# Joint softmax statistics in block 1's attention and two-pass state updates in the gated linear attention of a two-block model

## Chip, cores and metric

One core of one Trainium2 chip. The metric is the device time of one execution in microseconds (us), the median of three runs. TensorE (PE) multiplies, VectorE (DVE), ScalarE (ACT) and GpSimd (POOL) work on tiles of 128 partitions, and SyncE (SP) issues the DMAs.

## The reference, cut to what matters

The whole model is a first block (FFN, a mixer of sliding-window attention beside a state-space model, FFN) and a second one (multi-head latent attention, conv-FFN, gated linear attention or GLA, conv-FFN) on 512 tokens of width 1024. The change touches two places. In block 1's attention each query block of 128 tokens sees 16 meta keys and a band of 256 keys, with one sink score per head in the softmax:

```python
q = (q * (HEAD_DIM ** -0.5)).reshape(b, l, N_KV_HEADS, Q_PER_KV, HEAD_DIM)
sc = jnp.einsum('bqkgd,bskd->bkgqs', qn, keys).astype(jnp.float32)
p = sink_softmax(sc, mask, sink)          # softmax over the scores and one sink per head
```

In GLA (4 heads, key width 128, value width 256, 8 chunks of 64 tokens) each chunk updates a state and is read with it:

```python
upd = jnp.einsum('bnchk,bnchv->nbhkv', k_dec, v).astype(jnp.float32)
state = state * g[..., None] + u
return state, jnp.einsum('bchk,bhkv->bchv', qc, state)
```

## The kernel before

Activations lie transposed, features on partitions and tokens along the row. Every large product is made in three matmuls of a type that PE takes in one pass (fp32r): operands are split into a high half, rounded to that type, and a low half, the rest. `fetch` loads a weight tile `raw` on SP's queue, makes `whi` on ACT (L86) and `wlo` on DVE (L66); `wload` hands the next one out, out of rings of five. `proj` (L182) multiplies 512 or 2 x 264 tokens, and `nat` (L198) makes 128 tokens x 256 features: 24 matmuls of 256 columns, which this text calls a chunk of projection. Small products (scores, transposes, states) take plain fp32 operands.

The instructions of each engine are put in order by a scheduler when the program is built; PE, ACT, DVE, POOL and SP then run their own lists in order.

Block 1's attention (from L700): `query` evacuates a projection and scales it by 1/8 and by the token's norm factor `Rr`. A unit is two key heads (`pp`) with four query heads each and one block of 128 queries, eight units in all. `scores1` makes eight score matmuls (L727), evacuates each with a reduction that adds the mask and takes the row maximum (L730), and then, head by head, the maximum with the sink, its negative, the sink's exponential, four exponentials, the sum, its reciprocal and the scaling. `turn1` transposes (L759, L769), `values1` multiplies with the values (L781, L785). The quarters of the state-space model (`ssm_quarter`, L569 to L592) are woven in.

GLA (from L1286): `keys` makes `ek` in place, decayed keys of 128 tokens (two chunks of 64) x 512; `values` evacuates each 128 x 256 piece into `gv` with one copy. `recur` walks a head's four blocks `b`: two state updates (L1370), one for each chunk `c`, with 64 rows of `ek` against 64 rows of `gv`, into two PSUM banks; then the states `S` on DVE (L83) and the reading of each with the queries `gq` (L1381), which here is called the S matmul. The generators in `fill` make the next head's projections between the steps.

Of the kernel before, what the change touches and what calls it, by code (L numbers as in the profile page):

```python
# [53 lines left out]
def body(nc, tc, A, out, es):  # L54
# [10 lines left out]
    def tt(o, a, b, op, e=None):  # L65
        return (e or V).tensor_tensor(o, a, b, op=op)  # L66
# [581 lines left out]
    with tc.tile_pool(name="m1", bufs=1) as mp:  # L648
        att = mp.tile([P, 8, S], F32, name="att")
        with tc.tile_pool(name="m2", bufs=1) as ap_:  # L650
# [65 lines left out]
            def scores1(u):  # L716
# [6 lines left out]
                st = [[sm.tile([P, 4], F32, name=f"at{j}{s_}", bufs=2) for j in range(3)] for s_ in range(2)]  # L723
                for i in range(4):
                    pq = [pss("q"), pss("q")]
                    for s_ in range(2):
                        last["sc"] = PE.matmul(pq[s_][:, :W], qf[pp * 4 + i][:, n * P:(n + 1) * P],  # L727
                                               kw[pp][s_][:, max(n - 1, 0), :W])
                    for s_ in range(2):
                        V.tensor_tensor_reduce(sc[s_][:, i, :W], pq[s_][:, :W], mk, 1.0, -3.0e38,  # L730
                                               ALU.add, ALU.max, st[s_][0][:, i:i + 1])
                for s_ in range(2):
                    mx, dn, nb = st[s_]
                    t = sc[s_]
                    kv = 2 * pp + s_
                    sk = sink[:, kv * 4:kv * 4 + 4]
                    tt(mx, mx, sk, ALU.max)
                    ts(nb, mx, -1.0)
                    sub(mx, sk, mx)
                    act(mx, mx, AF.Exp)  # L740
                    for i in range(4):
                        act(t[:, i, :W], t[:, i, :W], AF.Exp, bias=nb[:, i:i + 1], accum_out=dn[:, i:i + 1])
                    add(dn, dn, mx)
                    V.reciprocal(dn, dn)
                    mul(mt[:, :, 32 * s_:32 * s_ + NM], t[:, :, :NM], dn.unsqueeze(2).to_broadcast([P, 4, NM]))
                    if s_:
                        for i in range(4):
                            act(t[:, i, NM:W], t[:, i, NM:W], AF.Copy, scale=dn[:, i:i + 1])
                    else:
                        mul(t[:, :, NM:W], t[:, :, NM:W], dn.unsqueeze(2).to_broadcast([P, 4, W - NM]))  # L750
                live[u] = sc, mt

            def turn1(u):
# [532 lines left out]
    with tc.tile_pool(name="g1", bufs=2) as mp:  # L1286
# [22 lines left out]
        for t, m in zip(L, lm):  # L1309
            act(t, t, AF.Ln, bias=1.0)  # L1310
            sub(t, m, t)
        ek = []
        for b in range(4):
            p = pss("s")
            PE.matmul(p, gc[:, 0:P], half(L, b))
            t = mp.tile([P, S], F32, name=f"ek{b}", bufs=1)
            act(t, p, AF.Exp)
            ek.append(t)
        pd = pss("s")
        for b in range(4):  # L1320
            for hh in range(4):
# [12 lines left out]

        def queries(i):

            t = qt[i] = mp.tile([P, 4, 2, P], F32, name=f"gq{i}", bufs=1)
# [4 lines left out]
            yield  # L1342

        def values(i):
            t = vt[i] = mp.tile([P, 4, 256], F32, name=f"gv{i}", bufs=1)
            return token("gla_v", lambda b, p: act(t[:, b], p, AF.Copy))

        def keys(c):
            return token("gla_k", lambda b, p: mul(ek[b][:, c * 256:(c + 1) * 256], ek[b][:, c * 256:(c + 1) * 256], p))

        def gates(hh):
            g = rg[hh] = mp.tile([P, 4, 256], F32, name="rg", tag="rg", bufs=4)
# [9 lines left out]
        def recur(hh):  # L1362
# [3 lines left out]
            for b in range(4):  # L1366
                pu = [pss("u"), pss("u")]
                for c in range(2):
                    rows = slice(64 * c, 64 * c + 64)
# [15 lines left out]
        def normalise(hh):  # L1385
            st4 = mp.tile([P, 4, 6], F32, name="st4")
            mv = mp.tile([P, 4, 2], F32, name="mv")
            nm = mp.tile([P, 4], F32, name="nm")
            o = ob[hh] = mp.tile([P, 4, 256], F32, name="ob", bufs=4)
# [188 lines left out]
```

## Time and profile before

| | |
|---|---|
| median of three runs | 2582.53 us (2582.31 to 2583.71) |
| the profiled execution | 2580.72 us, of which its span is 2578.9 us |
| PE busy | 2558.5 us, 99% of the span |
| DVE busy | 1577.0 us, 61% |
| ACT busy | 993.6 us, 39% |
| granted TensorE clock, mean | 0.999 |

Busy time of PE is made of matmul records whose ends are modelled and which overlap: a 256-column matmul's record lasts 0.28 us, while the next one starts 0.12 us later. What one matmul costs is read from the distance between starts.

### The profile page before, as it was taken

The numbers are of one execution on the slowest core, as the hardware profiler recorded it, in microseconds if no ns is written. First come the engines' busy times: TensorE is split into PE (matmuls) and PEld (weight loads), VectorE is DVE, ScalarE is ACT, GpSimd is POOL, SyncE is SP. The second block draws the span as 40 slices with busy tenths as digits, with TensorE's granted clock in tenths as the row PEclk, the third lists the DMA queues.
The fourth block names the chain that finished last, engine by engine and source line by source line (L and its number), as shares of the span: only waits on it lengthen the run. The fifth ranks groups of instructions, "written<-read, shape, count | busy, mean of one in ns | idle before, by whom it ended". The sixth has DMA issues, their size and how long they took to land.

```text
span 2578.9 us, 34903 instructions
## 1 busy us (share of the span) xinstructions
PE 2558.5 (99%) x13914; PEld 2181.4 (85%) x13914; DVE 1577.0 (61%) x2866; ACT 993.6 (39%) x1560; POOL 84.8 (3%) x98
## 2 busy tenths in 40 slices
PE   9999999999999999999999999999999999999999
PEld 9999999766888888888888888888878888888887
DVE  7985445685457544468665775555763457655566
ACT  5222223445333222236554454333353234433333
POOL 0000001000000000000000001000000010100000
PEclk9999999999999999999999999999999999999999
DMA  5443324332333333332112223333232222333332
GB/s 183 132 135 110 97 91 135 105 97 63 105 98 96 97 98 98 98 94 70 54 58 62 75 81 108 97 98 98 82 101 66 74 60 83 120 98 98 98 92 73
DMA packets 80774, 243.64 MB, mean 94 GB/s; under 512 B 10418, under 2 KB 20530, under 8 KB 80483
## 3 DMA queue, kind: packets, MB, share of 16 engines
q1 hardware_dynamic: 80610, 241.40, 30.8%
q8 instruction: 110, 1.80, 0.3%
q14 instruction: 54, 0.43, 0.1%
HBM read 229.44 MB, written 11.93 MB: 94 GB/s over the span
## 4 chain that ended last, share of the span: by engine, by line
PE 97%; DVE 2%; ACT 0%; issue 0%; DMA 0%; SPq 0%; DVEq 0%; ACTq 0%
PE ps_b L182 27%; PE ps_q L182 19%; PE ps_t L182 18%; PE mm L182 16%; PE ps_b L198 5%; PE ps_o L1240 1%; PE ps_q L1212 1%; PE ps_q L727 1%; PE ps_o L785 1%; PE ps_t L1228 1%; PE ps_q L1370 1%; DVE sq L66 1%; DVE h L66 0%; PE ps_t L769 0%; PE ps_b L1443 0%; PE ps_q L198 0%
## 5 line engine op out<-in xcount | busy, mean ns | idle before, releaser
L86 ACT ACTIVATE whi<-raw 128x1024 fp32r<-128x1024 f32 (+2 forms) x418 | 432.6, 1038 | 980.9 <-PE ps_b L182 276.3
L66 DVE TENSOR_TENSOR wlo<-raw,whi 128x1024 fp32r<-128x1024 f32 (+2 forms) x418 | 502.4, 1204 | 328.8 <-ACT whi L86 326.6
L182 PE MATMUL ps_b<-zh,whi 128*128 128x512 f32 (+1 forms) x692 | 272.9, 394 | 2.3 <-ACT att L86 0.7
L182 PE MATMUL ps_b<-zl,whi 128*128 128x512 f32 (+1 forms) x692 | 269.7, 390 | 0.0
L182 PE MATMUL ps_b<-zh,wlo 128*128 128x512 f32 (+1 forms) x692 | 269.1, 389 | 0.0
L182 PE MATMUL ps_q<-zh,whi 128*128 128x512 f32 (+1 forms) x488 | 189.3, 388 | 1.2 <-ACT zh L86 1.2
L182 PE MATMUL ps_q<-zl,whi 128*128 128x512 f32 (+1 forms) x488 | 189.4, 388 | 0.0
L182 PE MATMUL ps_q<-zh,wlo 128*128 128x512 f32 (+1 forms) x488 | 189.2, 388 | 0.0
L182 PE MATMUL ps_t<-zh,whi 128*128 128x512 f32 x476 | 185.6, 390 | 0.6 <-ACT zh L86 0.6
L182 PE MATMUL ps_t<-zl,whi 128*128 128x512 f32 x476 | 185.5, 390 | 0.0
L182 PE MATMUL ps_t<-zh,wlo 128*128 128x512 f32 x476 | 185.2, 389 | 0.0
L182 PE MATMUL mm<-zh,whi 128*128 128x264 f32 x800 | 162.5, 284 | 5.7 <-ACT whi L86 5.7
L182 PE MATMUL mm<-zl,whi 128*128 128x264 f32 x800 | 161.8, 284 | 0.0
L182 PE MATMUL mm<-zh,wlo 128*128 128x264 f32 x800 | 161.2, 283 | 0.0
L182 PEld LDWEIGHTS ps_b<-zh,whi 128*128 128x128 f32 (+1 forms) x692 | 129.2, 187 | 33.8 <-issue 2.5
L182 PEld LDWEIGHTS ps_b<-zh,wlo 128*128 128x128 f32 (+1 forms) x692 | 129.2, 187 | 28.6 <-issue 1.1
L182 PEld LDWEIGHTS ps_b<-zl,whi 128*128 128x128 f32 (+1 forms) x692 | 129.3, 187 | 27.2 <-issue 0.7
L182 PEld LDWEIGHTS mm<-zh,whi 128*128 128x128 f32 x800 | 124.3, 189 | 5.8 <-ACT whi L86 5.7
L182 PEld LDWEIGHTS mm<-zl,whi 128*128 128x128 f32 x800 | 124.1, 189 | 0.3 <-DVE zl L83 0.3
L182 PEld LDWEIGHTS mm<-zh,wlo 128*128 128x128 f32 x800 | 124.0, 189 | 0.0
L182 PEld LDWEIGHTS ps_q<-zh,whi 128*128 128x128 f32 x488 | 91.6, 188 | 20.8 <-ACT zh L86 2.0
L182 PEld LDWEIGHTS ps_q<-zl,whi 128*128 128x128 f32 x488 | 91.6, 188 | 20.4 <-DVE zl L66 1.3
(581 smaller groups left out, 5322.2 us busy)
## 6 DMA issues: line engine op xcount, KB each, us to landing
raw<-in_ffn_w_dram SPq DMA_DIRECT2D x130, 512.0 KB, 3.5
raw<-in_w_up_dram SPq DMA_DIRECT2D x88, 512.0 KB, 3.6
raw<-in_w_down_dram SPq DMA_DIRECT2D x44, 512.0 KB, 3.6
raw<-in_w_in_dram SPq DMA_DIRECT2D x32, 512.0 KB, 3.5
raw<-in_mla_o_dram SPq DMA_DIRECT2D x16, 512.0 KB, 3.6
raw<-in_ple_g_dram SPq DMA_DIRECT2D x16, 512.0 KB, 3.7
raw<-in_glu_dram SPq DMA_DIRECT2D x8, 512.0 KB, 3.5
raw<-in_w_out_dram SPq DMA_DIRECT2D x8, 512.0 KB, 3.5
```

Of the source, the lines that this page charges most:

```text
L66: return (e or V).tensor_tensor(o, a, b, op=op)
L86: return SC.activation(o, a, f, **kw)
L182: last["pe"] = PE.matmul(o[:, i, :c1 - c0], lhs, x[k][r][:, c0:c1], start=(k == 0 and j == 0), stop=(k == kt - 1 and j == 2))
L198: PE.matmul(o[:m, :n], x[k][a][:, t0:t0 + m], w[b][:, kk_ * c + m0:kk_ * c + m0 + n], start=(k == 0 and i == 0), stop=(k == kt - 1 and i = ...
L727: last["sc"] = PE.matmul(pq[s_][:, :W], qf[pp * 4 + i][:, n * P:(n + 1) * P], kw[pp][s_][:, max(n - 1, 0), :W])
L785: PE.matmul(po[64 * s_:64 * s_ + 64], vb[n - 1 + j][:, kv * 64:kv * 64 + 64], pT[s_][:, j], start=False, stop=(j == 1))
L1212: PE.matmul(p[:, :N], d["q"][e][:, bs], d["k"][e][:, :N], start=False, stop=True)
L1228: PE.transpose(pt[:, kt * P:(kt + 1) * P], sc[:, kt * P:(kt + 1) * P], ident)
L1240: PE.matmul(po[:, b * P:(b + 1) * P], vt[:, kt, e * P:(e + 1) * P], pT[:, kt * P:(kt + 1) * P], start=(kt == 0), stop=(kt == b))
L1370: PE.matmul(pu[c][:, :256], ek[b][rows, hc], vt[hh][rows, b])
```

## The change

Block 1. Four weight tiles (keys and values) are fetched ahead of the two key projections. A query is evacuated by an ACT copy with the factor 1/8; the token's norm factor moves into the reduction of the scores, as its factor `r`, and the sink moves in as the reduction's start value. The statistics of both heads of a unit lie in tiles of eight columns, and what follows (negative, exponential of the sink, sum, reciprocal) is done once for both; the maximum with the sink falls away.

GLA. The decayed keys are split: `kd[b][c]` holds, on the 64 partitions of chunk `c`, the high half, and on the other 64 the low half of the same keys. `gvh` holds the values' high half of chunk `c` on all 128 partitions (twice), and the low-half tile `gvl` (a ring of six that is zeroed once) has the low half on 64 partitions and zeros on the other 64. A state update is now two fp32r matmuls over 128 rows (L1399 of the changed program): `kd` against `gvh`, then against `gvl`. The queries' tiles `gq` become a ring of two, `ob` too.

```diff
+            for _ in range(4):
+                fetch("w_in", 1024)
             kw = []
...
-                stt(t, p[:, 0, :], 0.125, Rr, ALU.mult, ALU.mult)
+                act(t, p[:, 0], AF.Copy, scale=0.125)
...
-                        V.tensor_tensor_reduce(sc[s_][:, i, :W], pq[s_][:, :W], mk, 1.0, -3.0e38,
-                                               ALU.add, ALU.max, st[s_][0][:, i:i + 1])
+                        V.tensor_tensor_reduce(sc[s_][:, i, :W], pq[s_][:, :W], mk, r[:, n:n + 1], sk[:, c:c + 1],
+                                               ALU.add, ALU.max, mx[:, c:c + 1])
+                ts(nb, mx, -1.0)
+                sub(mx, sk, mx)
+                act(mx, mx, AF.Exp)
                 for s_ in range(2):
-                    mx, dn, nb = st[s_]
...
-                    tt(mx, mx, sk, ALU.max)
-                    ts(nb, mx, -1.0)
-                    sub(mx, sk, mx)
-                    act(mx, mx, AF.Exp)
                     for i in range(4):
...
-                    add(dn, dn, mx)
-                    V.reciprocal(dn, dn)
...
+                add(dn, dn, mx)
+                V.reciprocal(dn, dn)
...
+        kd = [[mp.tile([P, S], F32R, name=f"kd{b}{c}", bufs=1) for c in range(2)] for b in range(4)]
+        ch = lambda c: slice(64 * c, 64 * c + 64)
+        vl = [mp.tile([P, 2, 256], F32R, name=f"gvl{i}", bufs=1) for i in range(6)]
+        for t in vl:
+            for c in range(2):
+                ts(t[ch(1 - c), c], mask[ch(1 - c), :256], 0.0)
...
-            return token("gla_v", lambda b, p: act(t[:, b], p, AF.Copy))
...
+                for c in range(2):
+                    act(h_[ch(c), c], p[ch(c)], AF.Copy)
+                    act(h_[ch(1 - c), c], p[ch(c)], AF.Copy)
+                    sub(l[ch(c), c], p[ch(c)], h_[ch(c), c].bitcast(F32))
...
+                mul(t, t, p)
+                for c in range(2):
+                    k = kd[b][c][:, cols]
+                    act(k[ch(c)], t[ch(c)], AF.Copy)
+                    sub(k[ch(1 - c)], t[ch(c)], k[ch(c)].bitcast(F32))
...
-                    PE.matmul(pu[c][:, :256], ek[b][rows, hc], vt[hh][rows, b])
+                    for i, t in enumerate(vt[hh][b]):
+                        PE.matmul(pu[c][:, :256], kd[b][c][:, hc], t[:, c], start=(i == 0), stop=(i == 1))
```

Where the rows stand in the lists of the engines. On PE, in head 0's second block, the two updates and an S matmul before:

```order
L198 MATMUL ps_b<-whi,zl_16697 128x256
L198 MATMUL ps_b<-wlo,zh_16696 128x256
L1370 MATMUL ps_q<-gv_16801,ek_16772 128x256
L1381 MATMUL ps_o<-S,gq_16802 128x256
L1370 MATMUL ps_q<-gv_16801,ek_16772 128x256
L198 MATMUL ps_b<-whi,zh_16668 128x256
```

and in the third block now (L1410 is the S matmul):

```order
L198 MATMUL ps_b<-wlo,zh_16616 128x256
L1399 MATMUL ps_q<-gvh,kd_16706 128x256
L1410 MATMUL ps_o<-S,gq 128x256
L1399 MATMUL ps_q<-gvl_16712,kd_16706 128x256
L1399 MATMUL ps_q<-gvh,kd_16707 128x256
L1399 MATMUL ps_q<-gvl_16712,kd_16707 128x256
L198 MATMUL ps_b<-whi,zh_16588 128x256
```

Each update is a pair of rows now, and an S matmul still falls between updates. On DVE, at the passage from the conv-FFN to GLA, where `h_79` is the last piece of the activations and `zl` are the low halves of GLA's input, before:

```order
L83 SCALAR_TENSOR_TENSOR pg<-pg,pp_16344 128x512
L66 TENSOR_TENSOR h_79<-h_79,pg 128x512
L1297 MEMSET aT 17x512
L66 TENSOR_TENSOR zl_16685<-h_76,zh_16684 128x512
L66 TENSOR_TENSOR zl_16689<-h_77,zh_16688 128x512
L66 TENSOR_TENSOR zl_16693<-h_78,zh_16692 128x512
```

and now:

```order
L66 TENSOR_TENSOR h_79<-h_79,pg 128x512
L1299 MEMSET aT 17x512
L79 TENSOR_SCALAR gvl_16710<-mask 64x256 x2
L79 TENSOR_SCALAR gvl_16711<-mask 64x256 x2
L79 TENSOR_SCALAR gvl_16712<-mask 64x256 x2
L79 TENSOR_SCALAR gvl_16713<-mask 64x256 x2
L79 TENSOR_SCALAR gvl_16714<-mask 64x256
L66 TENSOR_TENSOR zl_16605<-h_76,zh_16604 128x512
L79 TENSOR_SCALAR gvl_16714<-mask 64x256
L79 TENSOR_SCALAR gvl_16715<-mask 64x256 x2
L66 TENSOR_TENSOR zl_16609<-h_77,zh_16608 128x512
```

The twelve zeroings of `gvl` stand ahead of and among the last four low halves. On SP, around the four projections of the state-space input (`uf`) and the keys', the list is the same in both programs:

```order
L156 DMA raw<-in_w_in_dram 128x1024 x2
L663 DMA u_d<-uf 32x4x132 x12
L156 DMA raw<-in_w_in_dram 128x1024
L550 DMA U<-u_d 128x528
L663 DMA u_d<-uf 32x4x132 x4
L156 DMA raw<-in_w_in_dram 128x1024 x9
```

(the line of the write is the changed program's L663 too). Nothing moved there, nor in ACT's list up to the evacuation of the first query.

## Rows read from the trace of the kernel before

**Rows 1.** The page, busy time by engine.

```profile
PE 2558.5 (99%) x13914; PEld 2181.4 (85%) x13914; DVE 1577.0 (61%) x2866; ACT 993.6 (39%) x1560; POOL 84.8 (3%) x98
```

**Rows 2.** Busy time by stage: window, its length, then each engine's busy us.

```profile
480.00:510.00 30.00, 26.57 (x142) 20.00 (x140) 27.87 (x105) 16.15 (x61) 1.16 (x3) 1.00 0.40 121
510.00:632.00 122.00, 119.79 (x566) 81.38 (x567) 87.16 (x243) 61.12 (x170) 2.61 (x7) 1.00 0.27 81
1912.00:1965.00 53.00, 53.00 (x323) 42.27 (x322) 22.62 (x29) 30.57 (x43) 2.08 (x8) 1.00 0.31 91
1965.00:2105.00 140.00, 140.00 (x964) 123.16 (x964) 66.40 (x156) 38.64 (x69) 11.08 (x15) 1.00 0.23 68
2154.00:2158.00 4.00, 4.00 (x16) 3.26 (x15) 1.29 (x8) 1.19 (x2) 0.00 (x0) 0.57 0.01 2
```

**Rows 3.** Waits of PE, 441 to 632 us: total, times, longest.

```profile
PE ps_b L591 <- DVE sq L66: 2.0, 2, 1.3
PE ps_b L569 <- DVE sq L66: 1.0, 1, 1.0
```

**Rows 4.** Timeline of PE around a lone update: start, duration.

```profile
1963.28 0.28 PE L198 MATMUL ps_q<-whi,zl 128*128 128x256 f32 x1
1963.39 0.28 PE L198 MATMUL ps_q<-wlo,zh 128*128 128x256 f32 x1
1963.60 0.70 PE L1370 MATMUL ps_q<-gv,ek 64*128 64x256 f32 x2
1964.23 0.39 PE L198 MATMUL ps_b<-whi,zh 128*128 128x256 f32 x1
1964.45 0.28 PE L198 MATMUL ps_b<-whi,zl 128*128 128x256 f32 x1
```

**Rows 5.** The same around two updates in a row.

```profile
1980.08 0.70 PE L1370 MATMUL ps_q<-gv,ek 64*128 64x256 f32 x4
...
1980.93 0.28 PE L198 MATMUL ps_b<-whi,zl 128*128 128x256 f32 x1
```

**Rows 6.** The same around a lone S matmul.

```profile
2091.25 0.28 PE L198 MATMUL ps_b<-whi,zh 128*128 128x256 f32 x1
2091.37 0.59 PE L1381 MATMUL ps_s<-S,gq 128*128 128x256 f32 x2
...
2091.91 0.28 PE L198 MATMUL ps_b<-wlo,zh 128*128 128x256 f32 x1
```

**Rows 7.** Groups by shape, 1912 to 2105 us: count, busy us, mean ns, idle before.

```profile
L198 PE MATMUL ps_b<-whi,zl 128*128 128x256 f32 x272 | 78.0, 287 | 0.0
...
L1370 PE MATMUL ps_q<-gv,ek 64*128 64x256 f32 x64 | 18.1, 428 | 0.0
...
L86 ACT ACTIVATE gv<-ps_b 128x256 f32<-128x256 f32 x13 | 4.9, 378 | 31.5 <-PE ps_b L198 31.5
...
L66 DVE TENSOR_TENSOR ek<-ek,ps_b 128x256 f32<-128x256 f32 x5 | 2.1, 414 | 3.4 <-PE ps_b L198 3.4
```

**Rows 8.** Groups of DVE by shape, 470 to 632 us.

```profile
L83 DVE SCALAR_TENSOR_TENSOR q<-ps_b,R 128x512 f32<-128x512 f32 x6 | 4.1, 687 | 9.4 <-PE ps_b L182 9.4
...
L66 DVE TENSOR_TENSOR at<-at,sink 128x4 f32<-128x4 f32 x16 | 2.3, 158 | 0.1
...
L80 DVE TENSOR_SCALAR y<-y 128x512 f32<-128x512 f32 x4 | 1.7, 416 | 0.0
```

**Rows 9.** Groups of ACT by shape, 430 to 632 us.

```profile
L86 ACT ACTIVATE sc<-sc,at 128x272 f32<-128x272 f32 x48 | 24.4, 509 | 6.3 <-DVE at L79 6.3
...
L86 ACT ACTIVATE kw<-kf 64x256 f32<-64x256 f32 x4 | 1.4, 399 | 0.0
```

**Rows 10.** Timeline where the values' projection starts.

```profile
440.80 0.71 DVE L66 TENSOR_TENSOR kf<-mm,R 128x528 f32<-128x528 f32 x1 [3.50 <-PE mm L182]
...
441.65 0.28 PE L198 MATMUL ps_b<-whi,zh 128*16 128x256 f32 x1 [0.89 <-ACT whi L86]
```

**Rows 11.** Timeline of DVE at the passage to GLA.

```profile
1919.06 2.50 DVE L66 TENSOR_TENSOR zl<-h,zh 128x512 fp32r<-128x512 f32 x4
```

More of the change, by code (lines that the diff above doesn't have):

```diff
@@ L722, in scores1 @@
                 sc = [ap_.tile([P, 4, 272], F32, name="sc", bufs=4) for _ in range(2)]
-                st = [[sm.tile([P, 4], F32, name=f"at{j}{s_}", bufs=2) for j in range(3)] for s_ in range(2)]
+                mx, dn, nb = (sm.tile([P, 8], F32, name=f"at{j}", bufs=2) for j in range(3))
+                sk = sink[:, pp * 8:pp * 8 + 8]
                 for i in range(4):
@@ L729, in scores1 @@
                     for s_ in range(2):
-                        V.tensor_tensor_reduce(sc[s_][:, i, :W], pq[s_][:, :W], mk, 1.0, -3.0e38,
-                                               ALU.add, ALU.max, st[s_][0][:, i:i + 1])
-                for s_ in range(2):
-                    mx, dn, nb = st[s_]
-                    t = sc[s_]
-                    kv = 2 * pp + s_
-                    sk = sink[:, kv * 4:kv * 4 + 4]
-                    tt(mx, mx, sk, ALU.max)
-                    ts(nb, mx, -1.0)
-                    sub(mx, sk, mx)
-                    act(mx, mx, AF.Exp)
-                    for i in range(4):
-                        act(t[:, i, :W], t[:, i, :W], AF.Exp, bias=nb[:, i:i + 1], accum_out=dn[:, i:i + 1])
-                    add(dn, dn, mx)
-                    V.reciprocal(dn, dn)
-                    mul(mt[:, :, 32 * s_:32 * s_ + NM], t[:, :, :NM], dn.unsqueeze(2).to_broadcast([P, 4, NM]))
+                        c = s_ * 4 + i
+                        V.tensor_tensor_reduce(sc[s_][:, i, :W], pq[s_][:, :W], mk, r[:, n:n + 1], sk[:, c:c + 1],
[3 more added lines that the diff above has]
+                act(mx, mx, AF.Exp)
+                for s_ in range(2):
+                    for i in range(4):
+                        c = s_ * 4 + i
+                        act(sc[s_][:, i, :W], sc[s_][:, i, :W], AF.Exp, bias=nb[:, c:c + 1], accum_out=dn[:, c:c + 1])
+                add(dn, dn, mx)
+                V.reciprocal(dn, dn)
+                for s_ in range(2):
+                    t, d = sc[s_], dn[:, s_ * 4:s_ * 4 + 4]
+                    mul(mt[:, :, 32 * s_:32 * s_ + NM], t[:, :, :NM], d.unsqueeze(2).to_broadcast([P, 4, NM]))
                     if s_:
                         for i in range(4):
-                            act(t[:, i, NM:W], t[:, i, NM:W], AF.Copy, scale=dn[:, i:i + 1])
+                            act(t[:, i, NM:W], t[:, i, NM:W], AF.Copy, scale=d[:, i:i + 1])
                     else:
-                        mul(t[:, :, NM:W], t[:, :, NM:W], dn.unsqueeze(2).to_broadcast([P, 4, W - NM]))
+                        mul(t[:, :, NM:W], t[:, :, NM:W], d.unsqueeze(2).to_broadcast([P, 4, W - NM]))
                 live[u] = sc, mt
@@ L1335, in queries @@
         def queries(i):
-            t = qt[i] = mp.tile([P, 4, 2, P], F32, name=f"gq{i}", bufs=1)
+            t = qt[i] = mp.tile([P, 4, 2, P], F32, name="gq")
             v = proj(wload("gla_q", 1024), P, 0, z, CS)[:, 0].rearrange("p (b c t) -> p b c t", b=4, c=2)
@@ L1344, in values, with evac, keys @@
         def values(i):
-            t = vt[i] = mp.tile([P, 4, 256], F32, name=f"gv{i}", bufs=1)
-            return token("gla_v", lambda b, p: act(t[:, b], p, AF.Copy))
-        def keys(c):
-            return token("gla_k", lambda b, p: mul(ek[b][:, c * 256:(c + 1) * 256], ek[b][:, c * 256:(c + 1) * 256], p))
+            t = vt[i] = []
+            def evac(b, p):
+                h_, l = mp.tile([P, 2, 256], F32R, name="gvh", bufs=6), vl[(4 * i + b) % 6]
+                t.append((h_, l))
+                for c in range(2):
+                    act(h_[ch(c), c], p[ch(c)], AF.Copy)
+                    act(h_[ch(1 - c), c], p[ch(c)], AF.Copy)
+                    sub(l[ch(c), c], p[ch(c)], h_[ch(c), c].bitcast(F32))
+            return token("gla_v", evac)
+        def keys(i):
+            cols = slice(i * 256, i * 256 + 256)
+            def evac(b, p):
+                t = ek[b][:, cols]
+                mul(t, t, p)
[3 more added lines that the diff above has]
+                    sub(k[ch(1 - c)], t[ch(c)], k[ch(c)].bitcast(F32))
+            return token("gla_k", evac)
         def gates(hh):
@@ L1388, in normalise @@
             nm = mp.tile([P, 4], F32, name="nm")
-            o = ob[hh] = mp.tile([P, 4, 256], F32, name="ob", bufs=4)
+            o = ob[hh] = mp.tile([P, 4, 256], F32, name="ob")
             pv = lambda b: po[hh][b // 2][:, (b % 2) * 256:(b % 2) * 256 + 256]
```

1 line of the change is left out of this document (removed).

## The prediction

> **What bounds the kernel.** I read the page's busy times first. PE has matmuls in flight for 2558.5 of 2578.9 us [rows 1], so the end moves only with what PE executes and with its few waits; DVE and ACT count only where PE waits for them. Then the busy times by stage [rows 2]. In GLA, from 1912 to 2105 us, PE is busy for all of 193 us and waits for nothing, with DVE at 89 us and ACT at 69 us. In block 1's attention, from 480 to 632 us, PE lacks 3.4 us and 2.2 us, 5.6 us together, and in the first 30 us of it DVE is busy for 27.9: there DVE is nearly the bound. The waits by name [rows 3] say who is late: the state-space chain on DVE (L591 2.0 us, L569 1.0 us). Another 0.9 us stands where the values' projection starts [rows 10]. So the change can win in three ways: less matmul work in GLA, at most 5.6 us of waits in the attention, and that 0.9 us.
>
> **Part 1: the state updates.** Records overlap, so I price by distances between starts on PE's timeline. A lone update: from the last projection matmul before it to the second one after it 1964.45 - 1963.39 = 1.06 us [rows 4]; two 256-column steps of 0.12 us (1963.28 to 1963.39, and so all through a chunk) are not its own, which leaves 0.82 us. Two updates of one block in a row, on the two halves of the rows: from the first record to the second projection matmul after them 1980.93 - 1980.08 = 0.85 us [rows 5], and the lone one has the same, 1964.45 - 1963.60 = 0.85 us; so 0.82 us for both. A lone S matmul, with all 128 rows and also 256 columns in fp32: 2091.91 - 2091.25 - 0.24 = 0.42 us [rows 6]. The update's 64 records [rows 7], two for each matmul, are 32 updates; the timeline has 20 of them alone and 6 times two in a row, and where an S matmul stands beside one, the prices add. So before: 20 x 0.82 + 6 x 0.82 = 21.3 us.
>
> After, each update is two one-pass matmuls of 128 rows and 256 columns, the form of the projection beside it. The low bound is its step, 0.12 us: 64 x 0.12 = 7.7 us. The high bound is the dearest step of such a matmul in these rows, the first after a switch of type: 1964.45 - 1964.23 = 0.22 us [rows 4], and 64 x 0.22 = 14.1 us. I take the low one: in PE's new list the passes stand beside projection matmuls or each other, with the same type. The S matmuls remain, at 0.42 us each, with their switches inside. **Term: -13.6 us (bounds -13.6 and -7.2).**
>
> One rule speaks against this. The trace shows that two updates on different halves of the array take the time of one (0.82 us, [rows 4, 5]). The Trainium skill, "TensorEngine Tiling (Array Packing)", section "Theoretical Speedup", gives a contraction of at most 64 rows up to twice the speed by such packing; the change gives it up and multiplies by zeros. It also says (section "Key Properties") that a change of tiling mode drains the engine; the lone update's 0.82 us beside the S matmul's 0.42 us, for the same columns, agrees with a switching price. Only six pairs are packed here, so what is given up is little beside it.
>
> **Part 2: what the updates' operands cost.** A values chunk was evacuated by one ACT copy of 0.378 us [rows 7]. Now it takes four of 64 x 256 and two DVE subtractions of that size. The nearest rows are 0.399 us on ACT for 64 x 256 [rows 9] and 0.414 us on DVE from PSUM [rows 7]; half the partitions save nothing. So 16 chunks add 16 x (4 x 0.40 - 0.38) = 19.5 us to ACT and 16 x 0.83 = 13.2 us to DVE; 8 keys chunks add two copies and two subtractions, 6.4 and 6.6 us. In the 193 us of GLA, ACT comes to 95 and DVE to 109 us, both below 60%: on average this lies behind PE. What is queued behind it are weight splits, the states on DVE, and PSUM: a chunk's bank is held until its last subtraction, by my sum 4 x 0.40 + 0.41 = 2.0 us, while the next chunk keeps PE for 24 x 0.12 = 2.9 us in the other bank. That leaves 0.9 us for anything that stands ahead in a queue, so now and then a chunk will wait. Bounds: 0 and 24 chunks x 0.5 us = 12 us; the rows of before show no wait at all there, so I take +0.8 us.
>
> The twelve zeroings: between half of 0.416 us, if the time goes with columns, and 0.416 us [rows 8], so 0.2 to 0.4 us each. Nine stand ahead of the first of the last four low halves, which started at 1919.06 and took 2.5 us [rows 11]: they come 1.9 to 3.7 us later, the last three a little more. PE's list puts 14 values matmuls, 14 x 0.12 = 1.7 us, ahead of the first that needs a late one. So PE waits 0.2 to 2.0 us, or up to 3 us for the last; I take +0.7 us.
>
> **Part 3: block 1.** The fetch ahead changes nothing: the queues' lists there are the same in both programs. The 0.9 us it could aim at isn't a weight's either: PE starts at 441.65 us, right behind DVE's read of the last key projection, 440.80 + 0.71 = 441.51 us [rows 10], which frees the PSUM that the values' projection takes over. Term 0.
>
> The statistics: five kinds of small instruction, 16 each, become four kinds with 8 each, 48 fewer of 0.158 us [rows 8]: 7.6 us less on DVE. The query leaves DVE for ACT: 6 x 0.687 = 4.1 us less in this window, as much at most more on ACT, which has 77 of 152 us busy [rows 2]. So DVE goes from 115 to 103 us. What it wins is bounded by PE's waits, -5.6 us. What it may lose: head one now shares the sum and reciprocal with head two, so its scaling comes four exponentials later, 4 x 0.51 us and their sums [rows 9], over 2.0 us in each of eight units, unless PE has other work; the first transposes of a unit read both heads' meta keys and waited for both before too. The list puts the next unit's scores and a projection of 24 x 0.227 us between, so I don't count it. The DVE waits of rows 3 are in the state-space chain, which gets a freer queue but is reordered too. **Term: -1.5 us (bounds -5.6 and +4).**
>
> **The sum**, against the profiled execution: 2580.7 - 13.6 + 0.8 + 0.7 - 1.5 = 2567.1 us. That execution lies 1.8 us below the median of the runs, so **2569 us** for the median. One more thing moves by itself: at 2154 us, behind one-column matmuls of a norm, the clock was granted at 0.57 over 4 us [rows 2], the level of 1.2 GHz for most of it. Such a stretch costs under 2 us, and a shift of 13 us may lose it or add one; I leave it in the range.
>
> **The rivals.**
> (a) *Nothing gained, for the array's sake.* If a pass over 128 rows cost what the records suggest (0.287 us against 18.1/64 = 0.283 us, [rows 7]), or if lost packing doubled what half the passes save, the updates would come to 18 to 21 us again: 2580 to 2583 us. For it: busy time by group shows no difference between old and new form. Against: 272 such matmuls step by 0.12 us. The Trainium skill's page "TensorEngine Tiling (Array Packing)" ("Theoretical Speedup") would be at its strongest here, with a full factor of two lost; this chance is that rule's too. Chance 6%.
> (b) *A part eaten by evacuation.* PSUM waits of 0.2 to 0.4 us in each of 24 chunks, or passes at a higher step: 5 to 9 us back, 2574 to 2578 us. For it: only 0.9 us of cover a chunk. Against: DVE and ACT below 60%. 16%.
> (c) *Slower, by the same evacuation.* It decides from 0.6 us of wait a chunk (24 x 0.6 = 14.4 us eats the gain); when a weight split of over 1 us stands ahead each time, the bank is held 3.7 us or more, PE waits 0.8 to 1.0 us a chunk, 19 to 24 us: 2588 to 2593 us. Against: the new lists were laid so that splits stand between the chunks' copies. 6%.
> (d) *The attention gives more.* Its waits all but vanish, and the clock's stretch too: 2562 to 2565 us. 10%.
> (e) *As forecast:* 2565 to 2574 us. 62%.
>
> **How the numbers follow.** The predicted time is (e)'s. Its own range is 2565 to 2574; to leave out no more than 2 in 10 I go down to 2564 and up to 2577, which takes in most of (b) and the upper part of (d). A measurement of this kernel tells 0.2%, about 5 us, from no change. Faster by over 0.2% (below 2577.4): (e), (d) and most of (b), 0.86. Within 0.2%: (a) and the rest of (b), 0.08. Slower: (c), 0.06.
>
> **What would show it.** Right: L1399 records 0.12 us apart, lone S matmuls still 0.42 us, PE's idle time in GLA below 2 us, the wait at the values' projection still 0.9 us, DVE's busy time in the attention some 12 us less. Wrong: waits of PE named after `gvl`, `gvh` or `kd`; waits behind `zl` at the passage; waits of L759 or L769 for `at`. The prediction fails if PE has over 8 us of new waits.

## The result: 0.7% slower, and why not 0.5% faster

The changed kernel takes 2602.76 us (median, 2601.57 to 2603.6), beside 2583.12 us for the kernel before on the same chip: a ratio of 1.0072, 95% interval 1.0059 to 1.0085. The forecast was 2569 us, with 2564 to 2577 as its range, so the sign was wrong as well. The profiled execution has a span of 2601.49 us, 22.6 us more than before.

Busy time by engine on the page of the changed kernel, the line that answers to [rows 1]:

```profile
PE 2568.0 (99%) x13914; PEld 2183.9 (84%) x13914; DVE 1597.7 (61%) x2870; ACT 1022.2 (39%) x1624; POOL 86.2 (3%) x98
```

PE is again busy nearly all the time, and its busy time is what grew. That alone doesn't say why: waits, a lower clock and slower matmuls all end in this line. The windows below part them (the same view as [rows 2]; the clock is the third number from the end):

```profile
480.00:510.00 30.00, 25.74 (x127) 18.05 (x126) 25.59 (x80) 16.66 (x58) 1.15 (x3) 1.00 0.35 113
510.00:632.00 122.00, 115.05 (x536) 80.37 (x536) 84.59 (x207) 57.96 (x161) 2.61 (x7) 0.94 0.26 77
511.70:521.90 10.20, 8.96 (x23) 4.85 (x24) 5.32 (x14) 3.85 (x10) 0.00 (x0) 0.50 0.12 26
1953.00:1974.00 21.00, 18.07 (x94) 13.08 (x92) 11.58 (x16) 20.58 (x31) 0.00 (x0) 1.00 0.27 89
1982.90:1989.70 6.80, 6.80 (x34) 6.80 (x34) 1.26 (x3) 1.03 (x3) 0.00 (x0) 0.50 0.00 1
1994.00:2115.00 121.00, 118.26 (x911) 112.97 (x911) 77.79 (x180) 54.89 (x113) 11.42 (x17) 1.00 0.26 79
2200.00:2300.00 100.00, 100.00 (x439) 82.04 (x438) 63.26 (x76) 47.13 (x60) 12.45 (x9) 1.00 0.36 111
```

For two stretches that no group of the kernel before has, its own rows in the same view:

```profile
1930.00:1950.00 20.00, 20.00 (x105) 14.94 (x105) 8.71 (x9) 18.90 (x25) 0.00 (x0) 1.00 0.25 74
2200.00:2300.00 100.00, 100.00 (x443) 82.81 (x442) 60.98 (x74) 39.69 (x50) 10.88 (x8) 1.00 0.35 106
```

Three things are to be seen. In the attention PE lacks 4.3 and 7.0 us, where it lacked 5.6 us in all before [rows 2], and for 10.2 us the clock is at 0.50, the level of 1.2 GHz. On the way into GLA ACT is busy for 20.58 of 21 us while PE lacks 2.9 us, and later 6.8 us run at the half clock. And from 2200 to 2300 us, far from every edit, PE waits for nothing at the full clock and yet gets through 439 matmuls where it got through 443.

The waits of PE by name, whole run, in the view of [rows 3], with the edits' own picked out:

```profile
PE ps_t L771 <- ACT pTm L86: 4.0, 1, 4.0
PE ps_s L1318 <- ACT ek L86: 3.8, 1, 3.8
PE ps_b L569 <- DMA U<-u_d: 2.9, 1, 2.9
PE ps_t L761 <- DVE mt L66: 2.1, 2, 1.2
PE ps_t L1438 <- DVE ob L66: 1.6, 1, 1.6
...
PE ps_t L761 <- DVE at L66: 1.0, 1, 1.0
PE ps_b L198 <- DVE kf L66: 0.9, 1, 0.9
```

Cutting both timelines of PE at five places parts the 22.6 us (lengths in us; differences to the kernel before in brackets; each is the distance between two starts of records):

| stretch | before | after | e1_pad | e3_gla | e4_blk1 | e13_best |
|---|---|---|---|---|---|---|
| start to the attention's last values matmul | 629.3 | 640.4 (+11.1) | 637.8 (+8.6) | 629.1 (-0.1) | 638.3 (+9.1) | 628.1 (-1.2) |
| from there to GLA's first matmul (`gla_a`) | 1283.1 | 1294.0 (+10.9) | 1286.3 (+3.2) | 1284.7 (+1.6) | 1284.7 (+1.6) | 1286.3 (+3.2) |
| to the first state update | 51.2 | 59.2 (+8.0) | 58.9 (+7.7) | 58.2 (+6.9) | 52.8 (+1.5) | 54.1 (+2.9) |
| to the last state update | 133.5 | 118.3 (-15.2) | 120.9 (-12.6) | 120.9 (-12.6) | 133.5 (0) | 119.9 (-13.6) |
| to the end | 481.8 | 489.6 (+7.8) | 484.3 (+2.5) | 484.3 (+2.5) | 481.7 (-0.1) | 485.9 (+4.1) |
| span | 2578.9 | 2601.5 (+22.6) | 2588.2 (+9.4) | 2577.2 (-1.7) | 2591.0 (+12.1) | 2574.2 (-4.6) |

Of the waits, `pTm` and `ek` are the two large ones; `mt`, `at` and `ob` are new as well and smaller, and the wait for the DMA of `U`, 0.5 us before, is 2.9 us. The state updates gave what they should. The attention lost 11 us, the way into GLA 8 us, and the two stretches that hold next to nothing of the edits 19 us. The columns to the right belong to the experiments. Each ran beside the kernel before on its own chip, where that took 2582.2 to 2584.6 us in the median, and ratios are to these runs. Each column is one profiled execution, and these show a few more half-clock stretches of 3.4 or 6.8 us, each costing half its length, behind the one-column matmuls of the norms' sums and at a row of two-column matmuls on the way into GLA. Kernels that have GLA as it was show the latter too: 3.4 us in e2_shift and e4_blk1, 6.8 us in e5_query and e14_sink. So differences of 1.7 or 3.4 us in the table, on the way into GLA too, need not be the edits'.

### The profile page after: what moved, and what is told of

It reads as the page before. It is cut to its first block, busy times and chain, and to the rows that moved or that the text cites. A ratio compares the mean times of both kernels' runs of the same rounds, so it can differ in the third digit from the quotient of the medians.

```text
span 2601.5 us, 35011 instructions
## 1 busy us (share of the span) xinstructions
PE 2568.0 (99%) x13914; PEld 2183.9 (84%) x13914; DVE 1597.7 (61%) x2870; ACT 1022.2 (39%) x1624; POOL 86.2 (3%) x98
## 4 chain that ended last, share of the span: by engine, by line
PE 96%; DVE 2%; ACT 1%; DMA 0%; issue 0%; SPq 0%; DVEq 0%; ACTq 0%
PE ps_b L182 27%; PE ps_q L182 19%; PE ps_t L182 19%; PE mm L182 16%; PE ps_b L198 5%; PE ps_o L1242 1%; PE ps_q L1214 1%; PE ps_o L787 1%; PE ps_q L730 1%; PE ps_t L1230 1%; PE ps_t L771 1%; DVE sq L66 1%; PE ps_b L1472 0%; PE ps_t L198 0%; PE ps_q L1212 0%; PE ps_q L1213 0%
```

## Experiments

### The addresses

Twelve statistics tiles of four columns take 32 bytes of a partition each, six of eight columns take 32 bytes each as well: the pool of small tiles shrank by 192 bytes, and every tile allocated after it lies 192 bytes lower, the activations `zh` and `zl` among them, the moving operands of the large matmuls; the weights lie ahead of the pool and stay. Experiment e1_pad gives the changed kernel its bytes back, e2_shift takes them from the kernel before; in both the lists of all five engines are unchanged, row for row.

```diff
 # e1_pad
                 mx, dn, nb = (sm.tile([P, 8], F32, name=f"at{j}", bufs=2) for j in range(3))
+                sm.tile([P, 48], F32, name="pad", bufs=1)
 # e2_shift
-                st = [[sm.tile([P, 4], F32, name=f"at{j}{s_}", bufs=2) for j in range(3)] for s_ in range(2)]
+                both = [sm.tile([P, 8], F32, name=f"at{j}", bufs=2) for j in range(3)]
+                st = [[t[:, s_ * 4:s_ * 4 + 4] for t in both] for s_ in range(2)]
 # e8_plus64, e12_plus32: the kernel before and a pad of 16 or of 8 columns
+                sm.tile([P, 16], F32, name="pad", bufs=1)
 # e11_minus128: e2_shift and a pad of 16 columns
```

> The changed kernel, with one unused tile of 48 fp32 columns (192 bytes of a partition) in the pool of small tiles, so that every pool that follows lies at the addresses of the kernel before; the lists of all engines are the same, row for row, as in the changed kernel. Theory A (placement): in the changed kernel the statistics take 6 tiles of 32 bytes in place of 12, all later tiles lie 192 bytes lower, and this alone lengthens the steps of 512-column matmuls from 227 to about 229 ns. Then the steps come back to 227 ns here, 7344 x 2.2 ns = 16 us come back, less what is in the stretches with waits: about 2587 to 2589 us, 14 to 16 us below the changed kernel. Rival B (the longer steps are the work of what DVE, ACT or the DMAs do beside PE, or of the clock): nothing changes, 2603 us.

> The kernel before, with the statistics of two heads in halves of one 32-byte tile, so that the pool of small tiles is 192 bytes shorter and all later pools lie 192 bytes lower; the instructions and their order are those of the kernel before. Theory A (placement): steps of 512-column matmuls rise from 227 to about 229 ns, and the time by 14 to 17 us, to 2597 to 2600 us, with nothing else changed. Rival B: no change, 2583 us.

> The kernel before with one unused tile of 64 bytes in the pool of small tiles: all later pools lie 64 bytes higher; the instructions and their order are those of the kernel before. Theory M (what counts of the addresses repeats every 256 bytes, and 64 higher is the same place as 192 lower): the steps of 512-column matmuls are 229 ns again, +11 to +16 us, as with 192 bytes less. Rival N (something else in the lower placement): steps of 227 ns and no change.

> The kernel before with all pools behind that of the small tiles 128 bytes lower (192 less, 64 more); the instructions and their order are those of the kernel before. 192 lower and 64 higher gave steps of 229.06 and 229.07 ns in place of 227.07. If what counts repeats every 128 bytes: 227 ns, no change, 2581 to 2586 us. If it repeats every 256 bytes or more and only the old place is good: 229 ns, 2594 to 2597 us.

> The kernel before with all pools behind that of the small tiles 32 bytes higher; the instructions and their order are those of the kernel before. The moving rows of most 512-column matmuls then begin at a multiple of 256 bytes (73216 for the first) instead of 32 below one. If a row that begins on such a border is read faster or as fast: 227 ns or less, 2583 us or up to 15 us less. If it is only the distance to the old place that counts: 229 ns, 2594 to 2597 us.

Measured, with the mean step between starts of 512-column projection matmuls (over 7100 steps in each trace, those over 260 ns left out):

| kernel | later pools | step, ns | time, us | to the kernel before |
|---|---|---|---|---|
| before | 0 | 227.07 | 2583.1 to 2584.6 | 1 |
| after | -192 bytes | 229.05 | 2602.8 | 1.0072 (1.0059 to 1.0085) |
| e1_pad | 0 | 227.07 | 2590.5 | 1.0025 (1.0016 to 1.0035) |
| e2_shift | -192 | 229.06 | 2595.5 | 1.0042 (1.0027 to 1.0057) |
| e8_plus64 | +64 | 229.07 | 2595.6 | 1.0048 (1.0032 to 1.0065) |
| e11_minus128 | -128 | 232.81 | 2625.1 | 1.0157 (1.0142 to 1.0172) |
| e12_plus32 | +32 | 233.29 | 2626.4 | 1.0162 (1.0146 to 1.0177) |

The window of 2200 to 2300 us of e1_pad, and then that of e12_plus32:

```profile
2200.00:2300.00 100.00, 100.00 (x442) 82.80 (x442) 63.91 (x78) 45.74 (x58) 13.66 (x10) 1.00 0.37 114
```

```profile
2200.00:2300.00 100.00, 100.00 (x430) 80.35 (x429) 64.63 (x81) 46.30 (x59) 10.70 (x8) 1.00 0.34 106
```

Theory A, that the addresses lengthen the steps, is shown both ways, and rival B fell: 192 bytes given back take 13.3 us off the span (2601.49 to 2588.22; 12.2 us off the median), 192 bytes taken from the kernel before cost it 0.42%, 11 us. Both are somewhat less than was expected (14 to 16 and 14 to 17 us). 7344 such matmuls at 2 ns more are 14.6 us, which is about that. Theory M, a repeat every 256 bytes, holds as far as it was tried: 64 higher is as 192 lower. Of the outcomes expected for e11_minus128 and e12_plus32 none came: that the period is 128 bytes fell with the first, that a row which begins on a border of 256 bytes is read as fast or faster fell with the second, the dearest of all (233.29 ns, 42 us), and the 229 ns expected otherwise came in neither.

### The two parts alone

> The kernel before with the GLA part of the change alone (two-pass updates, operands, zeroings); addresses ahead of GLA are those of the kernel before. Theory A: the recurrence gives 15 us (13.6 forecast), the way into it loses 8 us (waits of 4 us and two half-clock stretches behind them): 2575 to 2577 us. Rival C (the loss on the way into GLA comes from the later, disturbed state that block 1 and the addresses leave, not from GLA's own edits): 2567 to 2569 us, as the prediction had it for this part. Rival D (the longer steps are due to the GLA part): 2583 us or more.

> The kernel before with block 1's part of the change alone, and 192 unused bytes in the pool of small tiles, so that addresses are those of the kernel before. Theory A: the attention loses 11 us by itself (waits of PE and half-clock stretches behind them) and nothing else changes: 2593 to 2596 us. Rival E (what the attention shows is made good later or is an effect of the addresses): 2581 to 2585 us.

e3_gla: 2579.95 us, ratio 0.9983 (0.9973 to 0.9992), 3 us above what theory A gave. The updates' gain is there (12.6 us), and 6.9 us of it is lost on the way in, without block 1 or the addresses; 3.4 of these are two half-clock stretches, the second at the two-column matmuls. C and D fell. Its waits of PE in GLA, by name:

```profile
PE ps_s L1316 <- ACT ek L86: 3.4, 1, 3.4
...
PE ps_t L1436 <- DVE ob L66: 1.4, 1, 1.4
```

e4_blk1: 2596.16 us, ratio 1.0041 (1.0027 to 1.0054). Theory A again: the attention loses 9.1 us at unchanged addresses (11 were expected), and nothing of it is made good later, against E. The three parts together (0.42, 0.41 and -0.17%) make 0.66% of the 0.72% measured.

### The way into GLA

In the changed kernel's ACT timeline from 1948.6 to 1975.3 us one instruction follows the next: 16 of the 64 x 256 copies to `gvh`, where the kernel before had four copies in all, five weight splits, the decay's exponentials and logarithms with their table loads, and last the exponentials `ek` from 1974.23 on, for whose PSUM PE waits 3.8 us. Two half-clock stretches follow. The first, 3.4 us from 1976.04, begins 1.2 us after the wait's end. The second, 6.8 us from 1982.87, begins within the row of the decay's 32 two-column matmuls. e5_query (below) has GLA as it was and no wait of PE on the way in, and its clock does the same at that row. The row in the changed kernel, the row in e5_query, and the window behind it in e5_query:

```profile
1980.75 4.88 PE L1331 MATMUL ps_s<-gc,L 128*128 128x2 f32 x32
```

```profile
1955.79 4.81 PE L1324 MATMUL ps_s<-gc,L 128*128 128x2 f32 x32
```

```profile
1957.99:1964.82 6.83, 6.83 (x33) 6.83 (x33) 0.42 (x1) 0.20 (x1) 0.00 (x0) 0.50 0.00 0
```

Its way into GLA takes 54.3 us for 51.2 before. So the second stretch, 3.4 us lost, can't be put down to the edit. The kernel before and e9_dve have none there; what brings it was not found.

e7_pool takes half of the copies from ACT and the zeroings from DVE; the rest is the kernel before with the GLA part:

```diff
-                ts(t[ch(1 - c), c], mask[ch(1 - c), :256], 0.0)
+                GP.tensor_scalar(t[ch(1 - c), c], mask[ch(1 - c), :256], 0.0, None, op0=ALU.mult)
...
-                    act(h_[ch(1 - c), c], p[ch(c)], AF.Copy)
+                    GP.tensor_copy(h_[ch(1 - c), c], h_[ch(c), c])
```

> The kernel before with the GLA part, in which GpSimd makes the second copy of the values' high halves (from the first, SBUF to SBUF) and the twelve zeroings; ACT is left with two copies a chunk. Theory S (on the way into GLA ACT is the bound for 25 us, and the doubled copies put the decay's exponentials late): the wait at the decay matmul and the half-clock stretches behind it shrink from 7 us to 0 to 3 us, and the time falls to 10 to 14 us below the kernel before. Rival T (the loss comes from the zeroings' and subtractions' order, or GpSimd is too slow and the updates wait for it): no better than with the copies on ACT, 2 to 5 us below the kernel before or worse.

2576.26 us, ratio 0.9968 (0.9955 to 0.9981). Its waits of PE on the way in, and then its groups on GpSimd in GLA:

```profile
PE ps_s L1329 <- ACT ek L86: 0.2, 1, 0.2
PE ps_o L1316 <- ACT ek L86: 0.2, 1, 0.2
```

```profile
L1360 POOL CAST gvh<-gvh 64x256 fp32r<-64x256 f32 x32 | 16.5, 515 | 90.0 <-ACT gvh L86 89.2 <-DVE st L1419 0.5
...
L1325 POOL TENSOR_SCALAR gvl<-mask 64x256 fp32r<-64x256 f32 x12 | 11.7, 971 | 111.0 <-DVE h L66 110.3
```

Theory S, that ACT is the bound there, holds for the wait: `ek`'s goes from 3.4 to 0.4 us, though a copy takes GpSimd 515 ns and ACT 378; against T, no update waits for GpSimd. Copies and zeroings were moved together, so their shares are not parted. The time is 7.9 us below the kernel before, less than the 10 to 14 expected: 6.8 us at the half clock remain ahead of the first update, from 1960.12 on, again within the row of two-column matmuls. Beside e5_query, which has that stretch too, the way in is 1.3 us longer (55.6 us for 54.3).

### The attention

The wait of 4.0 us, on the changed kernel's timelines of PE and then of ACT:

```profile
507.87 0.60 PE L761 MATMUL ps_t<-ident,mt 128*64 128x128 f32 x4 [1.25 <-DVE mt L66]
508.30 0.60 PE L771 MATMUL ps_t<-ident,sc 128*128 128x128 f32 x4
512.94 1.11 PE L771 MATMUL ps_t<-ident,sc 128*128 128x128 f32 x4 [4.04 <-ACT pTm L86]
```

```profile
508.16 0.51 ACT L86 ACTIVATE sc<-sc,at 128x272 f32<-128x272 f32 x1
...
511.19 0.51 ACT L86 ACTIVATE sc<-sc,at 128x272 f32<-128x272 f32 x1
...
511.70 0.61 ACT L86 ACTIVATE y<-y 128x512 f32<-128x512 f32 x1
512.22 0.19 ACT L86 ACTIVATE at<-at 128x8 f32<-128x8 f32 x1
512.31 0.57 ACT L86 ACTIVATE pTm<-ps_t 64x512 f32<-64x512 f32 x1
```

The meta keys of a unit are transposed by 508.5 us, but the copy that frees their PSUM stands in ACT's list behind exponentials of the next unit and two more instructions. The kernel gives the transposes two banks of PSUM, so PE has no third to go on with. The Trainium skill has ACT's and DVE's queues as strictly first in, first out ("TensorE: Matmul & The Clock Gate", section "Architectural detail: the array is 16× 32×32, not 1× 128×128"); these rows agree: a copy that has its input at 508.5 us starts at 512.3, behind nine instructions. The half clock begins at 511.7, within PE's wait, and costs half of its 10.2 us.

The two halves of the edit were then tried alone (e5_query, e6_joined), the whole with the copy on DVE (e9_dve), and e6_joined with single pieces of the other half (e14_sink, e15_gpq); all stand at the addresses of before and have the fetch ahead:

```diff
 # e5_query: statistics head by head, but
-                stt(t, p[:, 0, :], 0.125, Rr, ALU.mult, ALU.mult)
+                act(t, p[:, 0], AF.Copy, scale=0.125)
-  mk, 1.0, -3.0e38,
+  mk, r[:, n:n + 1], sink[:, pp * 8 + s_ * 4 + i:pp * 8 + s_ * 4 + i + 1],
 # e6_joined: e4_blk1 with the query on DVE, mk, 1.0, -3.0e38, and
+                tt(mx, mx, sk, ALU.max)
 # e9_dve: e4_blk1 and
-                act(pTm, pm[:64], AF.Copy)
+                V.tensor_copy(pTm, pm[:64])
 # e14_sink: e6_joined without the maximum, and
+  mk, 1.0, sk[:, c:c + 1],
 # e15_gpq: e6_joined and
+                act(t, p[:, 0], AF.Copy, scale=0.125)
+                mul(t, t, Rr, GP)
```

> The kernel before with one half of block 1's change: the query is evacuated by ACT, and the norm factor and the sink go into the reduction of the scores; the statistics stay head by head, in tiles of four columns (only the maximum with the sink falls away). Addresses are those of the kernel before. Theory J (joining the statistics is what makes PE wait: no exponential of a unit can start before the last of its eight reductions, and no scaling before the last of its eight exponentials): this half costs little, the reductions being dearer (0.55 for 0.44 us) but the queries gone from DVE, between -2 and +3 us, 2581 to 2587 us. Rival Q (the dearer reduction, or the query on ACT, is the cause): +7 to +11 us, 2591 to 2595 us.

> The kernel before with the other half of block 1's change: statistics of both heads in tiles of eight columns and done once for both, the query on DVE with the norm factor and the reduction with its constants as before, and 192 unused bytes so that addresses are those of the kernel before. Theory J: the 4 us wait of a transpose for PSUM behind a row of exponentials on ACT, and a half-clock stretch behind it, are there: +7 to +11 us, 2591 to 2595 us. Rival Q: 2581 to 2585 us.

> Block 1's part of the change (both halves, at the addresses of the kernel before), with one edit more: the transposed meta keys' copy out of PSUM, pTm, is made by DVE instead of ACT. Theory J fell: either half alone costs the attention 1 us or nothing, both together 9 us, of which 4.0 us are one wait of a transpose for the PSUM that pTm's copy frees, behind eight exponentials of the next unit on ACT, and 5.1 us a half-clock stretch of 10.2 us that starts within that wait. Theory K (that one wait is the whole loss; ACT's list put the copy behind the joined exponentials): with the copy on DVE the wait and the stretch are gone, the attention ends 0 to 2 us later than in the kernel before, 2581 to 2586 us. Rival L (the joined unit is too long a chain, so a wait of this size stands at some other transpose or reading): 2590 to 2596 us.

> Joined statistics and the query on DVE with the norm factor, but the sink goes into the reduction as its start value, from a column of a tile, and the maximum with the sink falls away; addresses of the kernel before. Theory U (the reduction with an operand from a tile takes 0.55 in place of 0.44 us, and with the joined chain this makes DVE late for the transposes): the reduction takes 0.5 us or more here, the attention ends 2 to 9 us later than in the kernel before, 2585 to 2592 us. Theory V (the query's move to ACT, which lets the first scores come 6 us earlier in the lists, is what goes with the joining): the reduction may be dearer, but the attention ends within 2 us of the kernel before, 2581 to 2585 us.

> Joined statistics, the query evacuated by ACT and multiplied by the norm factor on GpSimd, the reduction with its constants and the maximum with the sink; addresses of the kernel before. Theory U: the reductions take 0.44 us, DVE has the queries off its list as well, and the attention ends at the same time as in the kernel before or up to 3 us earlier, 2578 to 2584 us. Theory V: it ends 4 to 9 us later, 2587 to 2593 us.

| kernel | start of the values' projection to the attention's last matmul, us | one 128x272 reduction, ns | ratio to the kernel before |
|---|---|---|---|
| before | 187.6 | 436 | 1 |
| e6_joined | 184.7 (-2.9) | 438 | 0.9990 (0.9981 to 1.0000) |
| e5_query | 188.8 (+1.2) | 555 | 1.0012 (1.0003 to 1.0021) |
| e15_gpq | 188.7 (+1.1) | 435 | 1.0022 (1.0012 to 1.0031) |
| e14_sink | 190.5 (+2.9) | 496 | 1.0018 (1.0009 to 1.0027) |
| e9_dve | 191.4 (+3.8) | 555 | 1.0022 (1.0012 to 1.0031) |
| e4_blk1 | 197.0 (+9.4) | 558 | 1.0041 (1.0027 to 1.0054) |

Theory J, that joining makes PE wait, fell: joined statistics alone are no loss but the one half that gains (2.9 us in the attention here and in e13_best; the interval of the ratio reaches 1.0000). Q, that the other half is the cause, fell as well, for that half alone costs the attention 1.2 us. e9_dve shows that the single wait, with its half clock and 1.3 us less of waiting for the DMA of `U`, is 5.6 of the 9.4 us; K's "whole loss" is too much, since 3.8 us stay (L, a wait of the old size elsewhere, fell), in waits of about 1 us each behind DVE, which now makes the copy as well, at the transposes:

```profile
PE ps_t L762 <- DVE mt L66: 1.9, 2, 1.0
...
PE ps_t L762 <- DVE at L79: 1.1, 1, 1.1
```

Neither U nor V holds alone: with joined statistics either piece of the other half turns the gain of 2.9 us into a loss of 2.9 (e14_sink, the dearer reduction, as U has it; 1.7 of it is a half-clock stretch at 495.4 us) or of 1.1 us (e15_gpq, the query off DVE, less than V has and against U; its factor is a GpSimd product of 1.9 us here, which the change doesn't have). That the two together, without the one wait, come to 3.8 us fits. The times say less than the attention does: e5_query (2588.4 us) and e9_dve (2589.0) lie between the ranges of both their theories, and in e15_gpq's profile half-clock stretches ahead of GLA and on the way into it make up 6.2 of the 7.3 us that its span is longer. Why the scheduler laid the one list with the 4 us wait only for the full combination was not tried.

The row of the reduction in the changed kernel, then in e6_joined, explains the dearer half:

```profile
L734 DVE CUSTOM_DVE_ANT_0 sc<-ps_q,mask,sink 128x272 f32<-128x272 f32 x48 | 25.7, 555 | 12.0 <-PE ps_q L730 11.0 <-PE ps_t L771 0.9
```

```profile
L735 DVE CUSTOM_DVE_ANT_0 sc<-ps_q,mask 128x272 f32<-128x272 f32 x48 | 20.4, 438 | 9.7 <-PE ps_q L731 9.2 <-PE ps_t L773 0.2
```

### The repaired kernels

e10_mended is the whole change with the pad, pTm's copy on DVE and GpSimd's copies and zeroings. e13_best leaves out the half of block 1 that loses: e6_joined with the GLA part of e7_pool.

> The whole change with three repairs: 192 unused bytes in the pool of small tiles, pTm's copy on DVE, and GpSimd for the values' second copies and the zeroings. If the three causes found (addresses, the wait in the attention, ACT on the way into GLA) are all that hid the gain of the updates, it is 8 to 13 us below the kernel before on the same chip, 2571 to 2576 us. If they act on each other and new waits come in: 2580 us or more.

> The joined statistics without the other half of block 1's change (query on DVE with the norm factor, reduction with its constants, maximum with the sink), the GLA part with GpSimd's copies and zeroings, and the addresses of the kernel before. If gains add: joined statistics alone measured 0.9990 of the kernel before, the GLA part so mended 0.9968; together 0.996, 10 to 11 us below the kernel before on the same chip. If they act on each other: 0.9975 or more.

e10_mended: 2578.89 us, ratio 0.9976 (0.9967 to 0.9986), 5 us below the kernel before and less than expected; its attention still ends 4.3 us late. e13_best: 2571.61 us, ratio 0.9958 (0.9943 to 0.9972), 10.6 us below the kernel before, as the gains add. It beats the kernel before and e10_mended. Its windows of the attention, of the way in and of the recurrence:

```profile
480.00:510.00 30.00, 27.66 (x147) 21.12 (x146) 27.99 (x94) 15.62 (x50) 0.84 (x2) 1.00 0.40 121
510.00:632.00 122.00, 120.79 (x583) 83.01 (x582) 85.11 (x220) 63.38 (x174) 2.92 (x8) 1.00 0.26 84
1914.00:1968.00 54.00, 54.00 (x311) 43.76 (x310) 27.49 (x41) 33.06 (x51) 17.55 (x24) 0.94 0.29 90
1968.00:2108.00 140.00, 138.33 (x1020) 131.93 (x1019) 87.12 (x205) 52.64 (x101) 25.19 (x44) 1.00 0.25 76
```

PE lacks 3.6 us in the attention, where it lacked 5.6 us [rows 2], and nothing on the way into GLA, where two half-clock stretches of 3.4 us stay (the mean clock is 0.94), as in e6_joined with GLA unchanged.

## Why the prediction was wrong, point by point

**Part 1, the updates (-13.6 us): right.** The two passes stand 0.12 us apart, a lone S matmul still takes 2107.15 - 2106.48 - 0.23 = 0.44 us. On the changed kernel's timeline of PE:

```profile
1993.47 0.28 PE L198 MATMUL ps_q<-wlo,zh 128*128 128x256 f32 x1
1993.59 0.28 PE L1399 MATMUL ps_q<-gvh,kd 128*128 128x256 f32 x1
1993.71 0.28 PE L1399 MATMUL ps_q<-gvl,kd 128*128 128x256 f32 x1
1993.83 0.29 PE L198 MATMUL ps_b<-whi,zh 128*128 128x256 f32 x1
...
2106.48 0.28 PE L198 MATMUL ps_b<-wlo,zh 128*128 128x256 f32 x1
2106.59 0.59 PE L1410 MATMUL ps_o<-S,gq 128*128 128x256 f32 x2
...
2107.15 0.28 PE L198 MATMUL ps_b<-whi,zl 128*128 128x256 f32 x1
```

From the first to the last update the changed kernel is 15.2 us shorter, e13_best 13.6 us. Some 2.5 us of that is other work which now stands behind the last update. Over all of GLA, from `gla_a` to the last transpose of the heads, e13_best takes 195.9 us for 204.1 before; with its 1.7 us of waits and 3.4 us for two half-clock stretches taken off, that is 13.3 us less. Rival (a) did not come about.

**Part 2, the operands (+0.8 us): this step failed.** "In the 193 us of GLA, ACT comes to 95 and DVE to 109 us, both below 60%: on average this lies behind PE." The average was true and the conclusion false. The first values chunks are evacuated on the way in, where ACT already had 18.90 of 20 us before (the row of 1930 to 1950 us above); the window of 53 us in [rows 2] had hidden it. There 12 copies more put `ek` late: a wait of 3.8 us and a half-clock stretch behind it (3.4 us, 1.7 us lost), 5.5 us for 0.8 forecast. The other stretch, 3.4 us lost, comes at the two-column matmuls in kernels with GLA unchanged too; the measured 8.0 us hold both, less some 1 us by which PE's other work there is shorter. The PSUM hold that the step feared, and rival (c) with it, costs next to nothing: no wait of a chunk's projection is over 0.5 us, here or in e7_pool. The large wait came with another name, `ek` in place of `gvl` or `kd`. The zeroings (+0.7 us) were sized about right: 311 ns each, and 0.4 us of waits behind `zl` in e3_gla, none in the changed kernel.

**Part 3, the fetch ahead (0): right.** The program with that edit alone, which was not run, has the lists of the kernel before on all engines, and in the changed kernel the 0.9 us wait is still there, now named after `kf`.

**Part 3, the statistics (-1.5 us, bounds -5.6 and +4): this step failed too**, and its bound. It counted 7.6 us of small instructions saved and took the reductions' price as unchanged. They went from 436 to 555 ns (48 of them) and from 300 to 423 (16): 5.7 + 2.0 = 7.7 us, all that was saved. DVE's busy time from 480 to 632 us fell by 4.9 us, not by 12. And "The list puts the next unit's scores and a projection of 24 x 0.227 us between, so I don't count it" put a wait at nothing that came: PE has no projection from 495 to 524 us, and the copy of the meta keys on ACT, which the term didn't look at, holds it for 4.0 us, with 5.1 us of half clock. In place of -1.5 us the attention takes 9.1 us more at the addresses of before (e4_blk1). For the joined statistics alone, which is not what the term was for, e6_joined measures -2.9 us.

**What the sum left out altogether.** The addresses: 13.3 us, more than any term but the first, mostly in stretches that the change doesn't touch. No step of the prediction looked at where tiles lie. Without them the miss would have been 2590 for 2569 us. The prediction's last sign of failing, over 8 us of new waits, came true on its own: 4.0, 3.8, 2.4 (`U`), 2.1, 1.6 and 1.0 us, 14.9 us together.

## What to carry to other kernels

Compare the addresses of all later tiles before and after an edit, even one of a few bytes, and pad back what moved: 192 bytes cost as much here as the faster updates gave. Read an engine's load in windows as short as the work that is moved there, about 20 us here and not 193, since the way into a stage can be full where its average is half. And price each edit of an operand's kind anew (a constant that becomes a column of a tile), and where an engine's list is laid by a scheduler, look again for what stands ahead of the copies that free PSUM. Before a few us between two profiles are put down to an edit, look whether a kernel without it shows the same stretch at the half clock.

## What the runs showed of the hardware

The step of an fp32r matmul of 512 columns changes with where the tiles behind the small ones lie in SBUF, with the same instructions. It is 227.07 ns where the moving rows of most stages begin 224 bytes behind a border of 256 (73184 for the first), 229.06 at 32, 232.81 at 96 and 233.29 at 0. That the moving rows are what counts is argued: of what these matmuls read they alone moved, but every other tile of those pools moved with them. Their place alone doesn't settle a step: from 2200 to 2300 us in e8_plus64 `zh` with `whi` takes 231.6 ns, `zl` with `whi` 226.0 and `zh` with `wlo` 229.1, and from 700 to 720 us 226.0, 229.0 and 231.7. The weights' tiles, which stayed, begin 224 bytes behind such a border too, so the distance between the two may be what counts; that was not tried. The Trainium skill gives 512 columns at the full clock 215.7 ns ("TensorE: Matmul & The Clock Gate", section "Wait — 56ns, not 53.3ns?"); no place tried here comes to that.

On DVE a reduction of 128 x 272 with its factor and start value as constants takes 438 ns, with one of them from a column of a tile 496 and with both 555: 58 and 59 ns more.

PE's clock was granted at 0.50 behind two kinds of event above all. One is a wait of 2.9 to 4 us inside a run of work (after, e1_pad, e3_gla, e4_blk1): the half clock begins within the wait or up to 1.2 us behind it, and lasts 3.4 us behind `U`'s and `ek`'s waits and 10.2 us behind `pTm`'s. The other is a row of narrow matmuls without such a wait: the 16 one-column matmuls of a norm's sum, as ahead of the window at 2154 us [rows 2], and the 32 two-column ones of GLA, behind or within which come 6.8 us in e5_query and e14_sink, 3.4 us in e2_shift and e4_blk1, and none in the kernel before. Such a stretch costs half of its length (in e5_query a 256-column step takes 0.21 us in it and 0.12 outside), 5.1 us for the wait of 4.0 us in the attention: more than the wait itself.
